# A softmax kernel gets a 16-byte store as ScalarE's first instruction

## The chip, the cores and the metric

The kernel runs on one core of a Trainium2 chip. Of the core's engines it uses VectorE (DVE) for maxima, reciprocals and products, ScalarE (ACT) for exponentials, GpSimd (POOL) for one copy and one late load, and SyncE (SP) to issue loads. All transfers between HBM and the on-chip buffer, whichever engine issues them, are carried out by the same 16 DMA engines. The metric is the device time of one execution in microseconds (us); lower is better.

## The reference

```python
def setup_inputs():
    batch, seq, dim = 16, 1024, 512
    return {
        "x": np.random.randn(batch, seq, dim).astype(np.float32),
    }

def reference(x: np.ndarray) -> np.ndarray:
    temp = 0.5
    x_scaled = x / temp
    x_max = np.max(x_scaled, axis=-1, keepdims=True)
    exp_x = np.exp(x_scaled - x_max)
    return (exp_x / np.sum(exp_x, axis=-1, keepdims=True)).astype(np.float32)
```

It is a softmax with temperature 0.5 over rows of 512 float32 values. There are 16,384 rows: 33.55 MB go in and 33.55 MB come out.

## The kernel before, in words

The 16,384 rows are cut into eight chunks (C = 8) of 128 partitions by 16 rows (G = 16) by 512 values, 4 MB each; one partition's share of a chunk is 32 KB in a row in HBM. Six tiles named `xt` hold chunks 0 to 5; chunks 6 and 7 reuse the tiles of chunks 0 and 1 once those are stored. Everything is done in place in `xt`.

A chunk is worked in blocks: chunk 0 in three (4, 4 and 8 rows), chunks 1 to 6 in one of 16, chunk 7 in two of 8. For a block:

- `shift` (lines 71 to 81) loads the chunk if it is not there yet (`load`, line 68, on SyncE's queue), takes the negated maximum of every row on VectorE (L77, tile `negmax`) and doubles it (L81, tile `bias`).
- `exponentials` (L108) runs one ScalarE instruction for each row: exp(2x + bias), with the row's sum gathered into `sums`.
- `scale_vector` (L125, L127) takes reciprocals of the sums and multiplies all rows but the last one or two on VectorE; `scale_scalar` (L138) multiplies those on ScalarE.
- `store` (L148) sends a finished chunk out, on ScalarE's queue, with one DMA of 4 MB. There are eight stores in all.

Chunk 0 is loaded in two parts, rows 0 to 3 (1 MB) and rows 4 to 15 (3 MB). Of chunk 7 the first 15 rows come on SyncE's queue; the last row comes on GpSimd's queue (`load_last_row`, lines 88 to 100), issued by GpSimd after it has copied one column of chunk 5's sums.

The order on each engine is written out by hand (`tc.manual_schedule()`): the loop over blocks runs the exponentials of block i + 1, the scaling of block i, the shift of block i + 2, and the store of block i. SyncE issues the loads of chunks 0 to 5 at once, and those of chunks 6 and 7 when the stores that free their tiles have landed. Completion of a DMA is told by a semaphore; the DMAs on the two hardware queues take eight semaphores in turn, so a DMA that takes one again waits first for that semaphore's earlier user. At the end SyncE waits for everything in the list `finished`, and then for the last store.

Before the loop a one-column tile `warm` is cleared by VectorE (L51) and put through the exponential by ScalarE (L52), which loads ScalarE's function table early. These are the first instructions of the two engines:

```python
    warm = stats.tile([P, 1], fp32, name="warm", bufs=1)
    nc.vector.memset(warm, 0.0)
    nc.scalar.activation(out=warm, in_=warm, func=EXP)
```

Of the kernel before, what the change touches and what calls it, by code (L numbers as in the profile page):

```python
# [1 line left out]

# [4 lines left out]


@with_exitstack
def kernel(  # L10
    ctx: ExitStack,
    tc: tile.TileContext,
    x: bass.AP,
    out: bass.AP,
):
    nc = tc.nc
    fp32 = mybir.dt.float32
    P = nc.NUM_PARTITIONS
    AX = mybir.AxisListType.X
    EXP = mybir.ActivationFunctionType.Exp  # L20
    COPY = mybir.ActivationFunctionType.Copy
    MAX = mybir.AluOpType.max

    D = x.shape[-1]
    xf = x.flatten_outer_dims()
    of = out.flatten_outer_dims()
    N = xf.shape[0]

    G = 16
    C = N // (P * G)
    assert C * P * G == N
    xr = xf.rearrange("(c p g) d -> c p g d", p=P, g=G)
    outr = of.rearrange("(c p g) d -> c p g d", p=P, g=G)
    WHOLE = [(0, G)]
    LOADS = [[(0, 4), (4, G)]] + [WHOLE] * 6 + [[(0, G - 1)]]
    BLOCKS = [[(0, 4), (4, 8), (8, G)]] + [WHOLE] * 6 + [[(0, 8), (8, G)]]
    STORES = [WHOLE] * 8  # L40
    BMAX = 16
    BUFS = 6

    data = ctx.enter_context(tc.tile_pool(name="data", bufs=BUFS))
    stats = ctx.enter_context(tc.tile_pool(name="stats", bufs=6))

    ctx.enter_context(tc.manual_schedule())


    warm = stats.tile([P, 1], fp32, name="warm", bufs=1)  # L50
    nc.vector.memset(warm, 0.0)  # L51
    nc.scalar.activation(out=warm, in_=warm, func=EXP)  # L52

    chunks = {}
    blocks = [(c, lo, hi) for c in range(C) for lo, hi in BLOCKS[c]]
    n = len(blocks)
    biases, sums, recips = {}, {}, {}

    finished = []

    def load(c):
        if c < BUFS:
            chunks[c] = data.tile([P, G, D], fp32, name="xt")
        else:
            chunks[c] = chunks[c - BUFS]
        xt = chunks[c]
        for lo, hi in LOADS[c]:
            part = nc.sync.dma_start(out=xt[:, lo:hi, :], in_=xr[c][:, lo:hi, :])  # L68
            finished.append(part.ins.name)

    def shift(i):
        c, lo, hi = blocks[i]
        if c not in chunks:
            load(c)
        b = hi - lo
        negmax = stats.tile([P, BMAX], fp32, name="negmax")
        nc.vector.tensor_reduce(  # L77
            negmax[:, 0:b], chunks[c][:, lo:hi, :], axis=AX, op=MAX, negate=True
        )
        biases[i] = stats.tile([P, BMAX], fp32, name="bias")  # L80
        nc.vector.tensor_scalar_mul(biases[i][:, 0:b], negmax[:, 0:b], 2.0)  # L81

    def load_last_row(signal):
        seen = stats.tile([P, 1], fp32, name="seen", bufs=1)
        copied = nc.gpsimd.tensor_copy(out=seen, in_=signal)  # L90
        finished.append(copied.ins.name)
        c = C - 1
        halves = "p (h d) -> p h d"
        to = chunks[c - BUFS][:, G - 1, :].rearrange(halves, h=2)
        of_ = xr[c][:, G - 1, :].rearrange(halves, h=2)
        for p0, p1 in ((P - 2, P), (0, P - 2)):
            part = nc.gpsimd.dma_start(  # L97
                out=to[p0:p1], in_=of_[p0:p1], max_dma_last_dim=2 * D
            )
            finished.append(part.ins.name)  # L100

    def exponentials(i, rows):
        c, lo, hi = blocks[i]
        if i not in sums:
            sums[i] = stats.tile([P, BMAX], fp32, name="sums")
        for g in rows:
            row = chunks[c][:, lo + g, :]
            nc.scalar.activation(  # L108
                out=row,
                in_=row,  # L110
                func=EXP,
                bias=biases[i][:, g : g + 1],
                scale=2.0,
                accum_out=sums[i][:, g : g + 1],
            )
            if c == BUFS - 1 and g == 10:
                load_last_row(sums[i][:, g : g + 1])


    def scale_vector(i):  # L120
        c, lo, hi = blocks[i]
        b = hi - lo
        k = b - b // 8
        recips[i] = stats.tile([P, BMAX], fp32, name="recip")
        nc.vector.reciprocal(recips[i][:, 0:b], sums[i][:, 0:b])  # L125
        rows = chunks[c][:, lo : lo + k, :]
        last = nc.vector.tensor_mul(  # L127
            rows, rows, recips[i][:, 0:k].unsqueeze(2).broadcast_to((P, k, D))
        )
        if i == n - 1:  # L130
            finished.append(last.ins.name)

    def scale_scalar(i):
        c, lo, hi = blocks[i]
        b = hi - lo
        for g in range(b - b // 8, b):
            row = chunks[c][:, lo + g, :]
            last = nc.scalar.activation(  # L138
                out=row, in_=row, func=COPY, scale=recips[i][:, g : g + 1]
            )  # L140
            if i == n - 1:
                finished.append(last.ins.name)

    def store(i):
        c, _, end = blocks[i]
        for lo, hi in STORES[c]:
            if hi == end:
                part = nc.scalar.dma_start(  # L148
                    out=outr[c][:, lo:hi, :], in_=chunks[c][:, lo:hi, :]
                )  # L150
                if c < C - 1:
                    finished.append(part.ins.name)

    shift(0)
    shift(1)

    def rows(i):
        c, lo, hi = blocks[i]
        cut = hi - lo - (2 if c == 1 else 0)
        return range(cut), range(cut, hi - lo)  # L160

    exponentials(0, rows(0)[0])
    for i in range(n):
        if i + 1 < n:
            exponentials(i + 1, rows(i + 1)[0])
        scale_vector(i)
        scale_scalar(i)
        if i + 2 < n:
            shift(i + 2)
        store(i)  # L170
        if i + 1 < n:
            exponentials(i + 1, rows(i + 1)[1])

    seen = nc.sync.nop()
    info = mybir.DependencyInfo(
        mybir.DependencyClass.Sync, mybir.DependencyReason.DATA
    )
    for name in finished:
        tc.add_manual_dep(seen.ins, name, info, reason="leaves one wait for the end")


# [1 line left out]
_INS = ['x']  # L183
_OUTS = [((16, 1024, 512), 'float32')]


# [23 lines left out]
```

## Time and profile before

| what | value |
|---|---|
| median of 3 runs | 161.76 us (161.74 to 162.32) |
| span of the profiled execution | 160.5 us |
| median less span | 1.25 us |
| VectorE busy | 134.6 us (84% of the span), 45 instructions |
| ScalarE busy | 102.2 us (64%), 273 instructions |
| GpSimd busy | 1.9 us |
| mean rate of all transfers over the span | 418 GB/s |
| first store issued | 44.10 us |
| last store issued | 147.48 us |

The span runs from the first to the last instruction of the profiled execution; what the runs' time has more lies around it and was not profiled, so the time of the profiled execution is taken as its span and the 1.25 us. "DMA share" in a stretch of time is the mean busy share of the 16 DMA engines. A packet's time and bytes are booked where the packet starts, and packets of a full chunk are 32 KB, so short stretches can show a share over 1. A queue's number tells who issues on it: q1 SyncE, q10 ScalarE, q0 GpSimd.

### The profile page before, as it was taken

The numbers are of one execution on the slowest core, as the hardware profiler recorded it, in microseconds if no ns is written. First come the engines' busy times: TensorE is split into PE (matmuls) and PEld (weight loads), VectorE is DVE, ScalarE is ACT, GpSimd is POOL, SyncE is SP. The second block draws the span as 40 slices with busy tenths as digits, with TensorE's granted clock in tenths as the row PEclk, the third lists the DMA queues.
The fourth block names the chain that finished last, engine by engine and source line by source line (L and its number), as shares of the span: only waits on it lengthen the run. The fifth ranks groups of instructions, "written<-read, shape, count | busy, mean of one in ns | idle before, by whom it ended". The sixth has DMA issues, their size and how long they took to land.

```text
span 160.5 us, 411 instructions
## 1 busy us (share of the span) xinstructions
DVE 134.6 (84%) x45; ACT 102.2 (64%) x273; POOL 1.9 (1%) x7
## 2 busy tenths in 40 slices
DVE  0607999999999999999999999999999999957000
ACT  3071549069989963998199909991899891790000
POOL 0000000000000000000000000030000000000000
DMA  5999999999989999999999999989999999999994
GB/s 184 470 408 498 400 392 457 457 392 402 506 269 425 490 392 400 506 400 392 490 425 392 474 434 392 490 383 483 422 450 400 400 465 441 392 457 449 400 441 204
DMA packets 2578, 67.13 MB, mean 418 GB/s; under 512 B 328, under 2 KB 328, under 8 KB 400
## 3 DMA queue, kind: packets, MB, share of 16 engines
q1 hardware_dynamic: 1296, 33.29, 49.3%
q10 hardware_dynamic: 1152, 33.55, 48.4%
q0 software_dynamic: 128, 0.26, 0.4%
q14 instruction: 2, 0.02, 0.0%
HBM read 33.55 MB, written 33.55 MB: 418 GB/s over the span
## 4 chain that ended last, share of the span: by engine, by line
DVE 75%; DMA 7%; issue 5%; ACT 3%; SPq 0%
DVE negmax L77 42%; DVE xt L127 31%; DMA xt<-in_x_dram 7%; ACT xt L108 3%; DVE bias L81 1%; DVE recip L125 1%; SPq L68 0%
## 5 line engine op out<-in xcount | busy, mean ns | idle before, releaser
L108 ACT ACTIVATE xt<-xt,bias 128x512 f32<-128x512 f32 x128 | 90.4, 708 | 41.5 <-DVE bias L81 40.6
L77 DVE TENSOR_REDUCE negmax<-xt 128x16 f32<-128x8192 f32 (+2 forms) x11 | 69.9, 6352 | 9.4 <-DMA xt<-in_x_dram 9.4
L127 DVE TENSOR_TENSOR xt<-xt,recip 128x7168 f32<-128x7168 f32 (+2 forms) x11 | 62.0, 5637 | 0.4
L108 ACT ACTIVATION_READ_ACCUMULATOR xt<-xt,bias 128x1 f32 x128 | 23.9, 187 | 0.0
L138 ACT ACTIVATE xt<-xt,recip 128x512 f32<-128x512 f32 x15 | 9.9, 706 | 0.0
L125 DVE RECIPROCAL recip<-sums 128x16 f32<-128x16 f32 (+2 forms) x11 | 2.4, 218 | 1.8 <-ACT xt L108 1.8
L81 DVE TENSOR_SCALAR bias<-negmax 128x16 f32<-128x16 f32 (+2 forms) x11 | 1.9, 173 | 0.4
L52 ACT ACT_TABLE_LOAD x1 | 1.3, 1283 | 0.7 <-PEq L194 0.7
L97 POOL DMA_DIRECT2D xt<-in_x_dram x2 | 1.5, 741 | 0.5 <-issue 0.5
L90 POOL COPY seen<-sums 128x1 f32<-128x1 f32 x1 | 0.2, 184 | 103.6 <-ACT xt L108 103.6
L51 DVE MEMSET warm<- 128x1 f32 x1 | 0.1, 59 | 0.8 <-PEq L194 0.8
L52 ACT ACTIVATE warm<-warm 128x1 f32<-128x1 f32 x1 | 0.2, 202 | 0.0
L194 POOL MEMSET const-float32-0.0<- 128x1 f32 x1 | 0.1, 93 | 0.2 <-issue 0.2
L194 POOL MEMSET const-bfloat16-1.0<- 128x1 bf16 x1 | 0.1, 95 | 0.0
L194 POOL MEMSET const-uint8-127<- 128x1 uint8 x1 | 0.1, 95 | 0.0
L194 POOL MEMSET const-float32-1.0<- 128x1 f32 x1 | 0.1, 93 | 0.0
## 6 DMA issues: line engine op xcount, KB each, us to landing
out_dram<-xt ACTq DMA_DIRECT2D x8, 4096.0 KB, 23.1
xt<-in_x_dram SPq DMA_DIRECT2D x6, 4096.0 KB, 34.8
xt<-in_x_dram SPq DMA_DIRECT2D x1, 3840.0 KB, 27.8
xt<-in_x_dram SPq DMA_DIRECT2D x1, 3072.0 KB, 11.6
xt<-in_x_dram SPq DMA_DIRECT2D x1, 1024.0 KB, 4.8
xt<-in_x_dram POOLq DMA_DIRECT2D x1, 252.0 KB, 15.4
xt<-in_x_dram POOLq DMA_DIRECT2D x1, 4.0 KB, 9.1
```

The lines of the kernel that those rows point to most:

```text
L51: nc.vector.memset(warm, 0.0)
L52: nc.scalar.activation(out=warm, in_=warm, func=EXP)
L77: nc.vector.tensor_reduce(negmax[:, 0:b], chunks[c][:, lo:hi, :], axis=AX, op=MAX, negate=True)
L81: nc.vector.tensor_scalar_mul(biases[i][:, 0:b], negmax[:, 0:b], 2.0)
L90: copied = nc.gpsimd.tensor_copy(out=seen, in_=signal)
L97: part = nc.gpsimd.dma_start(out=to[p0:p1], in_=of_[p0:p1], max_dma_last_dim=2 * D)
L108: nc.scalar.activation(out=row, in_=row, func=EXP, bias=biases[i][:, g : g + 1], scale=2.0, accum_out=sums[i][:, g : g + 1],)
L125: nc.vector.reciprocal(recips[i][:, 0:b], sums[i][:, 0:b])
L127: last = nc.vector.tensor_mul(rows, rows, recips[i][:, 0:k].unsqueeze(2).broadcast_to((P, k, D)))
L138: last = nc.scalar.activation(out=row, in_=row, func=COPY, scale=recips[i][:, g : g + 1])
L194: nc = _bacc.Bacc("TRN2", target_bir_lowering=False, num_devices=1)
```

## The change

Four lines are added. A tile `zeros` of 128 partitions by 4 float32 values is cleared by VectorE, ahead of `warm`. A tensor `first_store` of the same shape is made in HBM, and ScalarE stores `zeros` to it, ahead of its table load: 16 bytes for each of 128 partitions, 2 KB in all. Nothing reads `first_store`, and it is not in the list `finished`.

```diff
     warm = stats.tile([P, 1], fp32, name="warm", bufs=1)
+    zeros = stats.tile([P, 4], fp32, name="zeros", bufs=1)
+    nc.vector.memset(zeros, 0.0)
+    first = nc.dram_tensor("first_store", (P, 4), fp32)
+    nc.scalar.dma_start(out=first.ap(), in_=zeros)
     nc.vector.memset(warm, 0.0)
     nc.scalar.activation(out=warm, in_=warm, func=EXP)
```

The store waits for the memset of `zeros`. ScalarE's other instructions, and the loads and stores, keep their order. The new DMA takes a place in the rotation of the eight semaphores, so those of all later DMAs move by one.

## The prediction

> **What bounds the kernel now.** I read the DMA queues of the page first, then the chain of waits in order of time, then the busy time by stretches of 2 us, then the timeline of both ends. The queues (packets, MB, share of the 16 engines' span):
>
> ```profile
> q1 hardware_dynamic: 1296, 33.29, 49.3%
> q10 hardware_dynamic: 1152, 33.55, 48.4%
> q0 software_dynamic: 128, 0.26, 0.4%
> ```
>
> q1 carries SyncE's loads, q10 ScalarE's stores, q0 GpSimd's last row. Together the packets hold the 16 engines for 98.1% of 160.5 us: the transfers have about 3 us to spare, and those lie at the ends. The chain (start, length, what):
>
> ```profile
> 1.16 11.62 DMA xt<-in_x_dram
> 12.78 0.02 issue
> 12.80 2.30 DVE negmax L77
> ...
> 138.82 4.43 ACT xt L108 x13
> 143.24 0.02 issue
> 143.27 0.21 DVE recip L125
> 143.48 0.02 issue
> 143.50 3.89 DVE xt L127
> ```
>
> From 12.80 us VectorE follows itself, with ScalarE's last eight rows put in near the end, until the last product frees the last store at 147.4 us. So there are two bounds side by side. VectorE's chain hangs on the landing of the second load at 12.78 us; the DMA engines are full from the first load to the last store. An effect on the transfers at the start counts in both; one in the middle counts only in the second.
>
> Busy time by 2 us, where the last two columns are DMA share and GB/s:
>
> ```profile
> 0.00:2.00 2.00, 0.06 (x1) 1.26 (x1) 0.20 (x4) 1.00 0.33 53
> 2.00:4.00 2.00, 0.00 (x0) 0.22 (x2) 0.00 (x0) 1.00 0.81 315
> ...
> 42.00:44.00 2.00, 2.00 (x1) 2.00 (x6) 0.00 (x0) 1.00 1.10 475
> 44.00:46.00 2.00, 2.00 (x1) 1.55 (x5) 0.00 (x0) 1.00 0.78 311
> 46.00:48.00 2.00, 1.93 (x4) 1.73 (x6) 0.00 (x0) 1.00 1.09 262
> 48.00:50.00 2.00, 2.00 (x1) 2.00 (x7) 0.00 (x0) 1.00 1.07 459
> ```
>
> Divide share by rate: 1.10/475 and 1.07/459 are both 0.0023, and so is every stretch from 48 us to the end of the stores. Two places stand out. At 46 to 48 us, 262 GB/s should have needed a share of 0.61 and took 1.09, so each engine lost 0.48 x 2 = 0.97 us; at 44 to 46 us it lost another 0.06 x 2 = 0.12. That is **1.08 us on every engine**, once, just after the first store was issued at 44.10 us. None of the seven later stores shows it. At the start the same sum gives 0.41 us (0.33 against 0.125) and 0.13 us (0.81 against 0.745): **0.54 us**, where q1 is used for the first time. I read both as the price of the first use of a queue, larger on loaded engines than on idle ones.
>
> **The change part by part.** Nothing is removed. One VectorE memset, one ScalarE DMA of 128 packets of 16 bytes on q10, and one scratch tensor are added.
>
> ```profile
> 0.74 1.28 ACT L52 ACT_TABLE_LOAD   x1 [0.74 <-PEq L194]
> 0.74 3.53 SPq L68 DMA_DIRECT2D xt<-in_x_dram  x7
> 0.81 0.06 DVE L51 MEMSET warm<- 128x1 f32 x1 [0.81 <-PEq L194]
> ...
> 8.05 0.72 ACT L108 ACTIVATE xt<-xt,bias 128x512 f32<-128x512 f32 x1 [5.81 <-DVE bias L81]
> ```
>
> *Engines.* The memset of the zeros costs about 0.06 us (row L51) ahead of the old one; VectorE then idles until 5.52 us. ScalarE waits for it until about 0.9 us, issues for 0.34 us (the length of the other stores' issue), and its table load and warm exponential, 1.28 + 0.20 us, end near 2.8 us instead of 2.2. The first real exponential comes at 8.05 us after 5.81 us of idleness, so this costs nothing; without that cover it would be 0.5 us. Every later DMA also moves one place in the rotation of completion semaphores. In the built program the load of chunk 5 now waits on the semaphore of the first load, and SyncE issues it at about 5.5 us instead of 3.8. q1 still has four loads of 4 MB (some 9.7 us each) queued in front, so nothing is late; the last load and later stores wait only on transfers that landed long before. The wait at the end has the same semaphores.
>
> *The 128 packets, 8 for each engine.* No row has 16-byte packets on a hardware queue. From below: q0 moved 0.26 MB in 0.4% of the span, 0.64 us an engine, where 0.26 MB at the 433 GB/s of the middle stretches is 0.60 us, so its 56 tiny packets (328 under 512 B on the page, less 16 completions for each of 17 hardware DMAs) cost next to nothing: 0 us. From above: as if each were a packet of the first load (1,024 KB in 128 packets, 2.42 us at 433 GB/s, 0.30 us each): 8 x 0.30 = 2.42 us. I take 0.1 us, near the lower end, because time goes with bytes in all other packets here; both ends are kept.
>
> The Trainium skill, "DMA: Bandwidth & Descriptors" (section Specifications), speaks against that: under 512 B a DMA engine does a read-modify-write; the same page (section Latency and other measured facts) gives an HBM access 0.2 us. Estimated from this page, eight in series are 1.6 us, which would make the time about 163.0 us; no run here shows a 16-byte store, and the sum does not use it.
>
> *The stall at the start.* The new DMA is issued some 0.2 us after the first load. If its first use costs what it cost at 46 us, that is 1.08 us on engines that hold only the first loads; if it hides wholly in the load queue's own first use, 0. The nearest row is that other first use on idle engines, 0.54 us. The first load's packets are slow from 1.7 to about 2.5 us, and the new packets, issued near 0.95 us and needing the same 1.0 us (0.74 to 1.74 us) to arrive, fall inside that. So I take half of 0.54 as uncovered: 0.27 us. With the packets **x = 0.27 + 0.1 = 0.4 us** later landing of the second load (bounds 0 to 1.08 + 2.42 = 3.5). VectorE waits for that load, so its whole chain and the last store's issue move by x.
>
> *The stall at 46 us.* If it was the first use, it goes: 1.08 us off the transfers.
>
> *The end.* What can be gained there is limited by the last store's own issue:
>
> ```profile
> 147.48 0.34 ACTq L148 DMA_DIRECT2D out_dram<-xt  x1
> DMA to landing us min/median/max: 12.2/23.1/31.4
> xt<-in_x_dram SPq DMA_DIRECT2D x1, 1024.0 KB, 4.8
> ```
>
> The last store is the shortest, 12.2 us from issue to landing; its 4,096 KB at 433 GB/s are 9.69 us, leaving 2.5 us. The first load, with an empty queue in front, took 4.8 us: 2.42 of data, 0.54 of slow start, 1.84 of latency. So the last store stood 2.5 - 1.84 = **0.67 us** behind the store before it. The end therefore moves by the later of two: transfers, -1.08 + x; VectorE, -0.67 + x. With x = 0.4 these are -0.68 and -0.27, and the later decides: -0.27 us. The span goes from 160.5 to 160.2; the median has 1.25 us around the span (161.76 - 160.5), so 161.5 us. With x from 0.1 to 0.64 it is 161.2 to 161.7: VectorE's chain swallows 0.4 us of the gain whatever x is.
>
> **Rivals.**
> *The stall moves whole to the start.* For it: the cost was on every engine and nothing says that it needs load. Against: q1's first use was half as dear. x = 1.08 + 0.1 = 1.18; transfers +0.1, VectorE -0.67 + 1.18 = +0.51: 162.3 us.
> *The change doesn't do what it says.* The stall at 46 us belongs to the first large write of the output, or to the turn from loads alone to loads and stores, and stays. For it: queue, output tensor and direction are all new at 44 us, and no row parts them. Against: nothing but that order in time. Both bounds then keep what they have and x is added: the transfers decide at +x, 0.1 to 1.18 us: 161.9 to 162.9 us.
> *Small writes are dear: slower.* Eight 16-byte packets an engine stand in front of, or among, the second load's packets at up to 0.30 us each; x = 0.27 + 2.42 = 2.7, VectorE -0.67 + 2.7 = +2.0: 163.8 us. It decides for slower from x = 0.67 + 0.81 = 1.48 us, 0.15 us a packet. Against: the tiny q0 packets cost nothing visible; for: those are not writes to HBM.
>
> **How the numbers follow.** The forecast 0.45, the whole move 0.25, the stall that stays 0.15, dear small writes 0.15. A difference of 0.5% (0.81 us: 160.95 and 162.57) is what this measurement can tell. Faster by more needs a store that starts sooner than the 1.84 us of latency says, so that the transfers' -1.08 + x counts: 0.15, all from the forecast's case. Slower by more: nearly all of the dear writes, 0.14, and 0.05 to 0.06 each of the next two: 0.25. Within: 0.60. The time is that of the forecast's case, 161.5 (its own range 160.8 to 161.7, the lower end being x = 0.1 with the transfers alone deciding). For 8 in 10 the range reaches over the moved and the remaining stall into the dear writes: 160.8 to 163.0.
>
> **What would show it.** The 2 us stretch after the first large store at 0.0023 share per GB/s, as elsewhere, says that first use was the cause; 0.004 again, that it was not. VectorE's second reduce starting at 13.2 us (12.80 + 0.4) confirms x; 14.0 is the whole move, 15.5 the dear writes. The last store landing in 11.5 to 11.9 us after its issue, its queue empty in front, shows that VectorE's chain has become the only bound. I am wrong if the chain from 12.8 us is not rigid, or if the start of a used queue is much quicker than 1.84 us.

## The result, and the profile after

The changed kernel takes 162.51 us (median of 7 runs, 162.36 to 162.88) against 161.90 us before (7 runs, 161.74 to 162.32). The ratio is 1.0038, 95% interval 1.0025 to 1.0051: slower by 0.6 us, 0.4%. The forecast was 161.5 us, 0.3 us faster.

The later runs list the span of each execution beside its time, and that splits the 0.6 us in two. The seven runs of before have no such list, so 21 other runs of the same kernel stand for them:

| kernel | median time | median span | mean of time less span |
|---|---|---|---|
| before (21 runs beside the first experiments) | 161.85 | 160.1 | 1.77 |
| changed (7 runs) | 162.51 | 160.4 | 2.06 |

About 0.3 us lie within the span and 0.29 us around it. Before's profiled execution had a span of 160.5 us, which with 1.77 makes 162.28 us: of the three runs it was the slowest (162.32), and not the one at the median (161.76).

Within the span, the DMA issues of the changed kernel (KB each, us from issue to landing):

```profile
xt<-in_x_dram SPq DMA_DIRECT2D x1, 3072.0 KB, 12.5
xt<-in_x_dram SPq DMA_DIRECT2D x1, 1024.0 KB, 5.6
first_store<-zeros ACTq DMA_DIRECT2D x1, 2.0 KB, 5.6
```

The first load takes 0.8 us longer than before (4.8) to land, the second 0.9 (11.6). The tiny store takes as long as 1 MB. In the kept traces the first load's last data packet ends at the same time in both kernels (5.17 and 5.18 us): of this load only the completion comes later. The second load's last data packet ends at 13.31 us instead of 12.44, so there the packets themselves took longer. The chain of waits of the changed kernel in order of time:

```profile
1.16 12.49 DMA xt<-in_x_dram
13.65 0.02 issue
13.67 2.30 DVE negmax L81
...
144.36 3.89 DVE xt L131
```

The second reduce starts at 13.67 us, 0.87 later than the 12.80 of before, and the last product at 144.36, 0.86 later. Nothing was caught up. Now the changed kernel by stretches of 2 us (DMA share and GB/s last):

```profile
4.00:6.00 2.00, 0.00 (x0) 0.00 (x0) 0.00 (x0) 1.00 1.29 529
6.00:8.00 2.00, 1.68 (x1) 0.00 (x0) 0.00 (x0) 1.00 0.94 295
8.00:10.00 2.00, 0.78 (x2) 1.15 (x3) 0.00 (x0) 1.00 0.83 332
...
44.00:46.00 2.00, 2.00 (x1) 1.54 (x4) 0.00 (x0) 1.00 1.18 508
46.00:48.00 2.00, 1.93 (x4) 1.73 (x7) 0.00 (x0) 1.00 0.77 295
48.00:50.00 2.00, 2.00 (x1) 2.00 (x6) 0.00 (x0) 1.00 1.26 492
```

Undisturbed packets need a share of 0.00231 for each GB/s (1.00 for 433). At 6 to 8 us, 295 GB/s should have taken 0.68 and took 0.94. Before, the same stretch was clean, 418 GB/s in a share of 0.97:

```profile
6.00:8.00 2.00, 1.97 (x2) 0.00 (x0) 0.00 (x0) 1.00 0.97 418
```

From 4 to 12 us an engine loses 0.79 us this way in the mean of the 16; it was 0.06 before. At 44 to 52 us it still loses 0.43 us, where it was 1.10 before. So in these two executions part of the loss is gone from 46 us and a loss of the same kind stands at the start, where VectorE waits for it; `pool_clear`, below, shows how little of the sizes repeats. The end of the changed kernel:

```profile
148.34 0.34 ACTq L152 DMA_DIRECT2D out_dram<-xt  x1
DMA to landing us min/median/max: 11.1/22.7/31.4
```

The last store is issued 0.86 us later but lands in 11.1 us instead of 12.2. Hardly anything stands in front of it any more: in the kept trace the store before it ends 0.2 us after its first packet has started (149.37 and 149.18 us); in the kernel before it ends 1.0 us after it (149.51 and 148.47).

### The profile page after: what moved, and what is told of

The parts are those of the page before. It is cut to its first block, busy times and chain, and to the rows that moved or that the text cites. A ratio compares the mean times of both kernels' runs of the same rounds, so it can differ in the third digit from the quotient of the medians.

```text
span 160.3 us, 413 instructions
## 1 busy us (share of the span) xinstructions
DVE 134.6 (84%) x46; ACT 102.2 (64%) x273; POOL 1.9 (1%) x7
## 4 chain that ended last, share of the span: by engine, by line
DVE 75%; DMA 8%; issue 5%; ACT 3%; SPq 0%
DVE negmax L81 42%; DVE xt L131 32%; DMA xt<-in_x_dram 8%; ACT xt L112 3%; DVE bias L85 1%; DVE recip L129 1%; SPq L72 0%
```

## The experiments

"Start loss" and "46 us loss" are sums as above over 4 to 12 us and over 44 to 52 us, in the mean of the 16 engines, in the one execution profiled of each run; "reduce" is the start of the second reduce there. All times are in us. Each row was compared with runs of the kernel before on the same chip; their median span was 160.1 or 160.2 us.

| run | time | ratio (95% interval) | span | time less span | start loss | 46 us loss | reduce |
|---|---|---|---|---|---|---|---|
| again | 162.02 | 1.0004 (0.9992 to 1.0015) | 160.25 | 1.77 | 0.06 | 0.81 | 13.00 |
| two_memsets | 162.30 | 1.0018 (1.0005 to 1.0031) | 160.2 | 2.06 | 0.08 | 0.98 | 12.77 |
| warm_pool | 161.94 | 1.0000 (0.9990 to 1.0010) | 160.2 | 1.78 | 0.06 | 1.06 | 12.88 |
| no_dma | 162.18 | 1.0016 (1.0008 to 1.0025) | 160.1 | 2.07 | 0.06 | 0.95 | 12.98 |
| pool_clear | 162.20 | 1.0013 (1.0003 to 1.0022) | 160.4 | 1.77 | 0.42 | 0.81 | 13.21 |
| tiny_load | 162.39 | 1.0040 (1.0025 to 1.0054) | 160.3 | 2.06 | 0.16 | 0.79 | 12.99 |
| late_store | 162.49 | 1.0033 (1.0023 to 1.0043) | 160.4 | 2.06 | 0.07 | 0.88 | 13.09 |
| late_to_out | 162.44 | 1.0030 (1.0016 to 1.0044) | 160.35 | 2.07 | 0.06 | 0.75 | 13.01 |
| mid_to_out | 162.30 | 1.0022 (1.0012 to 1.0032) | 160.5 | 1.78 | 0.07 | 1.01 | 12.88 |
| to_out | 163.24 | 1.0082 (1.0070 to 1.0094) | 161.2 | 2.07 | 1.70 | 0.01 | 14.44 |
| to_out_end | 162.77 | 1.0051 (1.0032 to 1.0070) | 160.75 | 2.04 | 1.39 | 0.01 | 14.36 |
| out_128x16 | 162.77 | 1.0050 (1.0034 to 1.0067) | 161.0 | 1.77 | 1.39 | 0.01 | 14.31 |
| out_16x16 | 162.72 | 1.0043 (1.0029 to 1.0058) | 160.9 | 1.80 | 1.26 | 0.02 | 14.33 |
| rows_512 | 162.67 | 1.0044 (1.0029 to 1.0059) | 160.9 | 1.78 | 0.13 | 0.72 | 13.16 |
| out_512 | 162.32 | 1.0024 (1.0010 to 1.0038) | 160.5 | 1.79 | 0.13 | 0.80 | 13.27 |
| out_128x256 | 162.44 | 1.0033 (1.0018 to 1.0048) | 160.65 | 1.77 | 0.14 | 0.94 | 12.96 |
| out_16 | 161.81 | 1.0001 (0.9992 to 1.0009) | 160.0 | 1.79 | 0.09 | 0.79 | 12.95 |
| out_1 | 161.82 | 1.0001 (0.9992 to 1.0010) | 160.0 | 1.79 | 0.07 | 0.84 | 12.83 |

### What is paid around the span

`no_dma` is the changed kernel without its store; it keeps the tile, its clearing and the scratch tensor, and drops the store:

```diff
-    nc.scalar.dma_start(out=first.ap(), in_=zeros)
```

> The scratch tensor is declared and the zeros are cleared, but nothing is stored: the stall of 1.08 us after the first large store is back and the span that of the kernel before, 160.5 us. If the mere tensor is paid outside the span, time less span is about 2.1 us and the time 162.6 us; if it takes a DMA to it, 1.25 us and 161.8 us.

It has 2.07 us around the span without any DMA to the tensor. But `to_out` (below), which has no scratch tensor, also has 2.07. What these share is the memset. Next come the control, `again`, in which lines of the kernel before are moved down and nothing else, and `two_memsets`, the kernel before with one memset more:

```diff
     nc.vector.memset(warm, 0.0)
+    nc.vector.memset(warm, 0.0)
```

> The kernel before, with its lines moved down and nothing else: a control, and a second profile of it. If what lies around the span depends on the instructions, time less span is that of the runs of before, 1.77 us; if any new build can shift it by 0.3 us, it may be 2.05 us here. Inside: if the stall after the first large store varies from one execution to the next, this profile shows another size than 1.08 us, nearer 0.5 us, as the median span of before (160.1 us, against 160.5 in the profiled execution) suggests.

> The kernel before with the clearing of the warm tile done twice: one VectorE instruction more, no new tile, no DMA. If one instruction more is what is paid outside the span, time less span is about 2.05 us and the time 162.1 to 162.2 us, as with the cleared tile without its store; if the new tile or tensor is paid, 1.77 us and 161.85 us. The span is 160.1 us in both cases.

The control has 1.77 us, one VectorE instruction more 2.06. The other direction is to clear a tile by GpSimd: `zeros` in the changed kernel (`pool_clear`, whose edit is shown) and `warm` in the kernel before (`warm_pool`):

```diff
-    nc.vector.memset(zeros, 0.0)
+    nc.gpsimd.memset(zeros, 0.0)
```

> The changed kernel with the zeros cleared by GpSimd instead of VectorE; the store stays ScalarE's first instruction. If it is VectorE's one instruction more that is paid around the span, time less span falls from 2.06 to 1.78 us while the span stays at 160.4 us: 162.2 us. If any added instruction is paid, it stays at 2.06 us and the time at 162.5 us. Inside, a second look at the early scratch store: stalls of 0.5 to 0.8 us an engine between 3.5 and 12 us, second reduce near 13.7 us, and 0.3 to 0.5 us left at 46 us, if these sizes repeat.

> The kernel before with the warm tile cleared by GpSimd: one VectorE instruction less. If each VectorE instruction is paid around the span, time less span falls to about 1.5 us and the time to 161.6 us; if 0.29 us is a step that is crossed by one instruction more, it stays at 1.78 us and the time at 161.9 us.

With the zeros cleared by GpSimd the changed kernel has 1.77 us around the span at the same 160.4 us of span: 0.29 us are back, by moving one instruction of 0.06 us. What is left against the kernel before is 0.13% (0.03 to 0.22%), the 0.2 us within the span. One VectorE instruction less than before gains nothing (1.78). So it is a step between before and one memset more, and the change crosses it. What the step is made of, no run shows.

### What stalls: the queue, the output, or the small write

`tiny_load` uses ScalarE's queue first for a load. Its edit against the changed kernel:

```diff
-    first = nc.dram_tensor("first_store", (P, 4), fp32)
-    nc.scalar.dma_start(out=first.ap(), in_=zeros)
+    first = xf[0:1, :].rearrange("o (p f) -> (o p) f", p=P)
+    nc.scalar.dma_start(out=zeros, in_=first)
```

> ScalarE's first instruction is a load of 16 bytes a partition from the input into the small tile; nothing is written to HBM early and no scratch tensor exists. Theory A, the cost at the start is the first use of the queue: the second reduce still starts at about 13.7 us and the stall after the first large store stays at some 0.4 us an engine. Theory B, the cost at the start is the tiny write to HBM, behind which the loads' completions wait: the second reduce comes back to 12.8 us. Theory C, the stall at 46 us belongs to the first write and not to the queue: it is 1.08 us again. Outside the span 1.25 us if the scratch tensor was the cause there.

Here 128 packets of 16 bytes on the same queue cost 0.16 us at the start. Its stretches:

```profile
6.00:8.00 2.00, 1.97 (x2) 0.00 (x0) 0.00 (x0) 1.00 1.03 442
...
44.00:46.00 2.00, 2.00 (x1) 1.57 (x4) 0.00 (x0) 1.00 0.76 328
46.00:48.00 2.00, 1.93 (x4) 1.71 (x7) 0.00 (x0) 1.00 1.51 492
```

At 6 to 8 us 442 GB/s need 1.02 and took 1.03: no stall. At 46 to 48 us 492 GB/s need 1.14 and took 1.51: the stall is there in full (0.79 us in all, 0.81 in the control), though the queue was used long before. The first use of the queue explains neither place.

The kept traces show which packets lose the time. Before, from the issue of the first store to 48.4 us, all packets are SyncE's loads; those that start between 45.2 and 47.2 us take up to 2.5 us instead of 1.21, and the store's own first packet starts only at 48.41 us, when the stall is over. The other runs that have the stall show nearly all of it ahead of that packet too. In the changed kernel the 16-byte packets take 9 ns each, 0.07 us for eight; here too the lost time lies in the load packets beside and behind them.

`to_out` writes the 16-byte packets to the output's first row instead of the scratch tensor, `to_out_end` to its last row. The edit of `to_out` against the changed kernel:

```diff
-    first = nc.dram_tensor("first_store", (P, 4), fp32)
-    nc.scalar.dma_start(out=first.ap(), in_=zeros)
+    first = of[0:1, :].rearrange("o (p f) -> (o p) f", p=P)
+    nc.scalar.dma_start(out=first, in_=zeros)
```

> The early 16-byte store goes to the first row of the output (overwritten later by the first chunk's store) and no scratch tensor exists. In the changed kernel the time less the span is 2.08 us (162.36 - 160.28), against 1.25 us before. Theory A, the scratch tensor is what is paid outside the span: time less span falls back to about 1.25 us, the span stays at about 160.3 us, and the time is about 161.55 us, 0.3 to 0.4 us under the kernel before. Theory B, the added instructions or the early use of the store queue are paid outside the span: time less span stays near 2.1 us and the time at about 162.4 us. Both expect the second reduce on VectorE at 13.7 us, as in the changed kernel.

> As the early 16-byte store to the first row of the output, but to its last row, 33.5 MB further on (the last chunk's store overwrites it). Theory A, the first write to the output as a whole makes the engines wait, wherever it falls: a stall of some 1.5 us an engine in the second load's packets, second reduce near 14.4 us, no stall at 46 us, time about 163.2 us. Theory B, only writes near the same addresses count: the stall at 46 us stays near 0.8 us, and the start costs what the store to the scratch tensor cost, second reduce near 13.7 us, or nothing.

Both stall for 1.4 to 1.7 us at the start, and nothing at all is left at 46 us, whether the bytes go to the first chunk's region or 33.5 MB further on.

The same small stores stand later in ScalarE's program in three runs: behind its first four exponentials (`late_store` to the scratch tensor, `late_to_out` to the output) or behind the last of chunk 0 (`mid_to_out`, output). The expectations place them near 11 and 28 us. The traces show them issued at 8.0 to 8.1 and at 23.9 us, while those exponentials still run, and their packets start at 11.4 to 12.0 and at 27.7 us:

> The scratch tensor and the 16-byte store stay, but ScalarE issues the store after its first four exponentials, near 11 us, behind the first load. Scratch tensor paid outside the span: time less span stays near 2.1 us. Early store paid outside: back to 1.25 us. Inside, if the first use of the queue takes some 0.9 us of the engines wherever it falls, the second load is still late and the second reduce starts at 13 to 13.7 us; if the cost came from the wait of the first load's completion behind the tiny write, the first reduce is back at 5.5 us (6.3 in the changed kernel).

> The 16-byte store goes to the first row of the output, issued by ScalarE after its first four exponentials, near 11 us. Theory A, the first write to the output stalls all engines whenever it comes: a stall of 1 to 1.5 us an engine between 12 and 24 us, none at 46 us, the second reduce back at 12.8 to 13.1 us, and a span of 160.1 to 160.5 us. Theory B, a tiny write in mid-stream waits without holding the loads, as the late store to the scratch tensor did: no stall anywhere, the span falls to the floor of VectorE's chain, 159.4 to 159.7 us, and the time, with 2.05 us around it, to 161.5 to 161.7 us.

> The 16-byte store goes to the output's first row, issued by ScalarE near 28 us, behind chunk 0's exponentials and ahead of the first large store at 44 us (zeros cleared by GpSimd). Theory A, what the early store does to the stall at 46 us wears off with time: the tiny store, landing some 3 us before the large one, takes the stall whole, 1 us between 28 and 42 us and none at 46 us. Theory B, the tiny store in mid-stream never takes it: 0.7 us or more stay at 46 us, as with the tiny store at 11 us. In both VectorE's chain starts at 12.8 to 13.1 us and the span is 159.9 to 160.5 us; time less span 1.78 us.

The chain starts early again (12.88 to 13.09 us), but the stall at 46 us stays, 0.75 to 1.01 us. The tiny stores to the output cost 0.61 us at 12 to 30 us and 0.43 at 30 to 44 (0.04 and 0.06 in the control, 0.22 and 0.13 in the execution of before); the late one to the scratch tensor 0.12, which is no more than the executions without it differ by. In mid-stream the small store buys nothing.

Then the size. In all of these runs the zeros are cleared by GpSimd, and the store is ScalarE's first instruction: 512 bytes a partition to a scratch tensor (`rows_512`) and to the output (`out_512`), 256 bytes (`out_128x256`), 16 packets of 512 bytes (`out_16`), one of 2 KB on a single engine (`out_1`), and 16-byte packets again, 128 of them (`out_128x16`) and 16, one for each engine (`out_16x16`, whose edit against the kernel before is shown):

```diff
+    zeros = stats.tile([P, 4], fp32, name="zeros", bufs=1)
+    nc.gpsimd.memset(zeros, 0.0)
+    first = of[0:1, 0:64].rearrange("r (q f) -> (r q) f", f=4)
+    nc.scalar.dma_start(out=first, in_=zeros[0:16, :])
```

> As that, but 512 bytes a partition (64 KB in all) go to a scratch tensor of that size. Theory A, writes of less than 512 bytes are what is dear at the start: the stall of 0.68 us in the second load's packets is gone and the second reduce starts at 12.9 to 13.1 us, late by the 0.15 us that 64 KB take. Theory B, it is the first write to HBM whatever its size: the stall stays at 0.5 us or more and the second reduce at 13.6 us or later.

> The early store goes to the first 32 rows of the output, 512 bytes a partition from 128 partitions, 64 KB in all (zeros cleared by GpSimd). Theory A, an early write to the output costs its 1.3 to 1.6 us of stall at the start whatever the size, and takes the stall at 46 us: second reduce near 14.4 us, span 161.1 us. Theory B, only writes under 512 bytes stall at the start, and the early write to the output still takes the stall at 46 us: second reduce near 13.1 us, no stall at either place, span at the floor of VectorE's chain, 159.5 to 159.8 us, time 161.3 to 161.6 us, under the kernel before. Theory C, without the stall at the start there is no gain at 46 us either: 0.7 to 1.0 us there, span 160.2 to 160.9 us.

> The same with 16 partitions of 512 bytes, one packet for each of the 16 engines, 8 KB in all, to the output's first four rows. As before: A, second reduce near 14.4 us and no stall at 46 us; B, second reduce near 12.9 us, no stall at 46 us, time 161.3 to 161.5 us; C, the stall at 46 us stays at 0.7 us or more and the time at 161.9 to 162.1 us.

> One partition of 2 KB to the output's first row: one DMA engine alone writes early. If what the first write pays is shared by all engines (the memory side of the output), the stall at 46 us is gone or halved on all of them, and the start costs that one engine at most; if each engine pays for itself, 15 of 16 engines still stall at 46 us, 0.7 to 1.0 us in the mean.

> One 16-byte packet for each engine (16 partitions) to the output's first row, zeros cleared by GpSimd. If each packet under 512 bytes has its price, the eight packets an engine that cost 0.3 to 1.6 us make 0.04 to 0.2 us here: second reduce at 12.9 to 13.1 us, the stall at 46 us stays, time 161.8 to 162.0 us. If the first small write pays once, whatever the number, the stall at the start is 0.5 us or more and the second reduce at 13.6 us or later.

> The 128 packets of 16 bytes to the output's first row once more, with the zeros cleared by GpSimd. If the sizes of the first time repeat, 1.3 to 1.6 us of stall an engine at the start, second reduce near 14.4 us, no stall at 46 us, span 161.1 us, and with 1.78 us around it 162.9 us. If they were chance, the stall at the start is 0.3 to 0.7 us and some stays at 46 us, as with the scratch tensor.

> 128 packets of 256 bytes to the output's first 16 rows. If it is being under 512 bytes that is dear, the stall at the start is as with 16 bytes, 0.7 to 1.6 us, and the second reduce at 13.7 to 14.4 us. If the price falls with the size, or comes from many packets falling into the same 2 KB, it is under 0.3 us and the second reduce at 12.9 to 13.2 us.

The pair that says most differs in packet size, and with it in the bytes covered (256 bytes against the first 8 KB of the output) and by 0.1 us in the issue: 16 packets of 16 bytes (`out_16x16`),

```profile
4.00:6.00 2.00, 0.00 (x0) 0.00 (x0) 0.00 (x0) 1.00 1.62 487
6.00:8.00 2.00, 1.02 (x1) 0.00 (x0) 0.00 (x0) 1.00 0.63 233
...
46.00:48.00 2.00, 1.93 (x4) 1.68 (x5) 0.00 (x0) 1.00 1.06 459
```

and 16 packets of 512 bytes (`out_16`), in the same stretches:

```profile
4.00:6.00 2.00, 0.16 (x1) 0.00 (x0) 0.00 (x0) 1.00 1.22 512
6.00:8.00 2.00, 2.00 (x1) 0.00 (x0) 0.00 (x0) 1.00 1.00 430
...
46.00:48.00 2.00, 1.93 (x4) 1.73 (x7) 0.00 (x0) 1.00 1.17 377
```

With 16 bytes, 487 GB/s took a share of 1.62 where 1.12 would do, and at 46 us 459 took the 1.06 that it needs. With 512 bytes the first rows are clean, and at 46 us 377 GB/s took 1.17 instead of 0.87. One small packet an engine costs as much as eight (1.26 and 1.39 us), so the price is paid once and not for each packet. Packets of 256 bytes cost 0.14 us, no more than those of 512. One rival is not tested: in every run with 16-byte packets these lie side by side (2 KB or 256 bytes in all); no run writes 16-byte packets far apart, and none has a size between 16 and 256 bytes. Three results are not explained. The runs with 128 larger packets have a span of 160.5 to 160.9 us, more than the 160.0 of `out_16` and `out_1`, with hardly any start loss in the execution profiled. `tiny_load` and `late_store` have spans 0.2 and 0.3 us over before's (160.3 and 160.4 against 160.1), nearly those of the changed kernel, without a stall at the start and with the whole one at 46 us. And the early small store to the scratch tensor pays only part (0.79 and 0.42 us) and leaves some or all of the stall at 46 us (0.43 and 0.81).

None of these versions beats the kernel before. `out_16` and `out_1` equal it: an early store that costs nothing also takes nothing away at 46 us.

## Why the prediction was wrong

**The two bounds held.** From the second reduce to the issue of the last store is 134.68 us before, 134.67 in the changed kernel and 134.67 to 134.71 in all other runs. Where the loss at 46 us is gone or more than halved, the span ends 11.92 to 12.04 us after that issue; elsewhere 12.4 to 13.2. So the span of the changed kernel's profiled execution is 13.67 + 134.67 + 11.94 = 160.28 us, and whatever delays the second load is paid in full.

**"VectorE then idles until 5.52 us", so the memset costs nothing:** wrong outside the span. The sum set the 1.25 us around it as a constant. They are 1.77 us, because the median was compared with a slower execution's span, and the added instruction makes them 2.06. This step alone is 0.29 us of the 0.6 us.

**x = 0.4 us at the start:** mis-sized for the execution profiled. x measured 0.87 us (13.67 against 12.80 us). It is not a steady size: `pool_clear`, the same store, has 0.41 us (13.21), and eight kernels with no small store or load at the start begin between 12.77 and 13.09. The term of 0.27 us, half of "the load queue's own first use", had the wrong cause: `tiny_load` uses the queue first and loses 0.16 us in all. Its overlap failed too: the new packets were to arrive near 1.95 us, inside the slow start of the first load's packets, and start at 3.47 us. That slow start stays in every run, 0.48 to 0.65 us from 0 to 4 us. The packets' 0.1 us was right for the packets themselves (0.07); what they do to the loads was put at nothing.

**"If it was the first use, it goes: 1.08 us off":** this is the step that failed in its mechanism. The stall that follows the issue of the first large store is not the first use of the queue (0.79 us with `tiny_load`), nor the first write to the output (0.79 to 0.94 us after early stores of 256 bytes and more). Its 1.08 us is a mean of the 16 engines, from a single execution. Early 16-byte packets to the output take it whole, and pay 1.26 to 1.70 us for it. The scratch store of the change took 0.67 us of it in the profiled execution, but 0.29 or less in `pool_clear`, the same store at nearly the same time (0.87 against 0.91 us); as the control loses the same 0.81 us there, it may have taken nothing.

**"-0.67 + x" at the end:** right in form. The 1.84 us of latency in it were too many: with its queue nearly empty the last store landed 11.1 us after its issue, 1.4 us more than the 9.69 us of its data, so it gained 1.09 us in the profiled pair (13.03 to 11.94 us from issue to the end of the span). With x = 0.87 that pair's span fell by 0.2 us, near the 0.27 us of the forecast, but by luck: two errors of 0.4 to 0.5 us that cancel. And the pair has before's longest execution in it, span 160.5; the median span is 160.1 us, and the floor is about 12.80 + 134.68 + 11.95 = 159.4 us, so a median run had some 0.7 us to gain. 0.87 - 0.7 gives 0.2 us, near the 0.3 us between the median spans; as x varies between executions and `tiny_load` and `late_store` reach nearly the same span by another way, this sum is argued and not shown.

**The rivals.** "Small writes are dear" came nearest: it had the size of the writes and the place, but priced it by the packet, 2.7 us in all. It is one price, paid by the loads beside them, 0.4 to 0.8 us of lost DMA time for the scratch tensor and 1.3 to 1.7 for the output. The Trainium skill, "DMA: Bandwidth & Descriptors" (section Specifications), sets its limit for read-modify-write at 512 B; the runs agree that 16 bytes are dear and 512 are not, but 256 bytes were not dear either, and no run here shows a read-modify-write. "The stall moves whole to the start" is what the 16-byte stores to the output do, at more than its price (1.26 to 1.70 us for the 0.72 to 1.10 that are gone). "The stall at 46 us stays" came true for every version that costs next to nothing at the start.

**The moved semaphores** cost nothing, as said: the load of chunk 5 was issued at 6.3 us, when the first load had landed (5.5 was forecast), and its queue stayed full.

What stays open is why one 16-byte packet an engine stalls the loads, whether their size or their lying side by side does it, what the loads wait for between the issue of the first large store and its first packet, why the small packets must come in the first microseconds to take that stall away, and why the scratch tensor pays only in part.

## What to carry to other kernels

Before moving a stall, look which chain waits at the new place: 1 us in mid-stream had buffers in front of it, and at the start it delayed a chain of 134.7 us that has no gap. Take the time around the span from runs that list both, never from a median and another execution's span; one instruction more can move it. A warm-up must be of the kind that takes the stall away, and here that kind cost more than it saved.

## What was not expected of the hardware

- One VectorE memset of 0.06 us adds 0.29 us around the span (1.77 to 2.06 us; 2.04 to 2.07 in all eight kernels that have it); on GpSimd it adds none.
- 16-byte writes to the output in the first microseconds hold up the loads of another queue: 1.26 us in the mean of the engines with a single packet for each, though a packet takes 9 ns itself. 16-byte reads do not (0.16 us with eight packets for each).
- Once, after the issue of the first large store and nearly all ahead of that store's first packet, the loads lose 0.72 to 1.10 us in the mean of the engines, in every run without a 16-byte store at the start; the sizes of the same kernel's stalls differ by 0.3 us between executions (1.10 and 0.81).
- A small store that stands behind exponentials in ScalarE's program is issued while they still run: at 8.1 us in `late_store`, where the fourth exponential ends near 11 us.
